# First norm of a fused decoder layer: token tile 0 normalised on VectorE, its first transposes between late output products, and the first FFN block's gate and up products by chunk

## The chip, the core and the metric

The kernel runs on one core of a Trainium2 chip. The core has five engines that work at the same time, each through its own list of instructions in order, and that wait for each other by semaphores: TensorE (PE in the rows) does the matrix products and transposes into PSUM banks, VectorE (DVE) and ScalarE (ACT) do elementwise work, GpSimd (POOL) does some more of it, and SyncE (SP) issues most DMAs. The metric is the device time of one execution in microseconds (us); lower is better. Times in rows are us from the start of the span.

## The reference, cut to what matters

One decoder layer for 256 tokens of width 1024, all in float32: a combined input projection, two groups of attention heads (latent attention and block-sparse attention), an output projection, a first layer norm, a gated FFN with a causal convolution over tokens, and a second layer norm.

```python
mix = jnp.concatenate([a_out, b_out], axis=-1) @ w_o[l]
x = layer_norm(alpha * x + mix, ln1_g[l], ln1_b[l])
x = layer_norm(alpha * x + conv_gated_ffn(x, w_up[l], conv_w[l], conv_b[l], w_down[l]), ln2_g[l], ln2_b[l])

def layer_norm(x, g, b):
    mu = jnp.mean(xf, -1, keepdims=True)
    var = jnp.mean(jnp.square(xf - mu), -1, keepdims=True)
    return (xf - mu) * lax.rsqrt(var + EPS) * g + b

def conv_gated_ffn(x, w_up, conv_w, conv_b, w_down):
    h = x @ w_up                      # 1024 -> 2 * 2816
    h = conv3_causal(h) + conv_b      # each channel over 3 tokens
    gate, up = jnp.split(h, 2, axis=-1)
    return (jax.nn.silu(gate) * up) @ w_down
```

## The kernel before, in words

The 256 tokens are two tiles of 128 (tile 0 and tile 1), the width is eight chunks of 128 columns (`k` from 0 to 7). Each float32 operand of a product is split into a high part (rounded to the fast format float32r) and a low part (what is left), and a product is the sum of three: high by high, low by high, high by low. For weights, `split` (lines 81 to 89) casts the high part on ScalarE and subtracts it on VectorE.

The stage that the change touches lies between the attention and the FFN. Its parts:

- **Output projection** (`gen_wo`, line 414; issued from line 484). The sums `pm` stand in four banks: tile 0 in two halves of 512 columns (`pm00`, `pm0512`), tile 1 likewise (`pm10`, `pm1512`). What is left at the end of attention are the "late" products: line 484 lists those of tile 1, first half of columns for `k` 4 to 7, then second half, and line 485 puts the last chunk of tile 0 (`k` 7, both halves in turn, six products) behind the first two of them.
- **First norm** (lines 495 to 536). For each tile and half, `ln_add` forms `alpha * x + pm` in `r` on VectorE and `ln_part` takes statistics of it; `ln_root` combines them (BN_AGGR on VectorE) and takes a square root on ScalarE; `ln_scale` inverts it on VectorE. Tile 0 is then normalised on ScalarE (lines 530 to 532), tile 1 on VectorE (lines 575 to 577). All of these are pinned: each engine runs them in the order in which they are written (`pin`).
- **Turning the tokens** (class `Turned`, line 538). TensorE transposes chunks of `r` into a bank `x1t`, four chunks to a bank for tile 0 (`a0` for chunks 0 to 3, `a4` for 4 to 7) and two for tile 1 (`tiles[0]` to `tiles[3]`, banks `x1t10`, `x1t12`, `x1t14`, `x1t16`). `affine` multiplies by the norm's gain and adds its bias, from the bank into `x1T` in SBUF, on ScalarE or VectorE; `high` casts `x1T` into the high part `x1hi` on ScalarE; `low` subtracts it into the low part `x1lo`, on GpSimd for tile 0 and on VectorE for tile 1. `keep_warm` puts five products of zeros in front of the transposes of tile 1.
- **FFN** (from line 608). Block `f` of 22 has a gate (`w` 0) and an up part (`w` 1), each with its bank `ph`. In the first block (`f` 0) the products are narrow: 256 columns of `x1hi` for each chunk, then those of `x1lo` (lines 613 to 619). From block 1 on, one product of 512 columns takes `x1hi` and `x1lo` of a chunk together (line 625). `down` (line 669) adds the block's share of the down projection into `pd`, two blocks later.

Except where pinned, a scheduler sets each engine's order in advance; for the first FFN blocks it mixes `ph00`, `ph01` and `ph10` by chunk as their inputs are due. TensorE takes its instructions in that order, so one that waits holds up all behind it.

## Time and profile before

| | |
|---|---|
| time, median of 3 runs | 308.75 us (308.45 to 310.67) |
| profiled execution | 309.6 us, its span 307.8 us |
| TensorE (PE) busy | 296.9 us, 96% of the span |
| VectorE (DVE) busy | 241.9 us, 79% |
| ScalarE (ACT) busy | 196.6 us, 64% |
| GpSimd (POOL) busy | 29.4 us, 10% |

The busy share is an average over stages. The page also slices the span in 40; TensorE shows nine tenths or more in every slice but the first and the last. So the stage in question, some 15 us around 110 us, is to be read from the list of instructions in order of time, engine by engine. In such a row the first number is the start, the second the time from the start of the first to the end of the last instruction of the row, then engine, line of the kernel, operation, what it writes and reads (tile names without their numbers), shape, and count; in brackets, if the engine stood idle before it, how long and for whom it waited. Neighbouring instructions overlap a little: the engine takes the next before the last one's result has landed.

### The profile page before, as it was taken

How to read it: one execution, taken by the hardware profiler on the slowest of the kernel's cores; microseconds unless marked ns; L12 is line 12 of the kernel's file. 1: busy time of each engine (PE TensorE's matmuls, PEld its weight loads, DVE VectorE, ACT ScalarE, POOL GpSimd, SP SyncE). 2: the span in 40 equal slices, each digit the busy share in tenths (PEclk: the TensorE clock that was granted, in tenths of full speed). 3: DMA queues.
4: the chain of work that ended last, by engine and by line, in shares of the span. 5: the costliest groups of instructions: out<-in, count | busy, mean ns of one | idle time of the engine just before them, and what ended most of it. 6: DMA issues, size and time to landing. Idle time of an engine off the chain costs nothing.

```text
span 307.8 us, 4769 instructions
## 1 busy us (share of the span) xinstructions
PE 296.9 (96%) x1672; PEld 258.9 (84%) x1672; DVE 241.9 (79%) x487; ACT 196.6 (64%) x386; POOL 29.4 (10%) x43
## 2 busy tenths in 40 slices
PE   8999999999999989999999999999999999999990
PEld 7987999889887869888888888888888888888890
DVE  2968888866755387999999888888886978975585
ACT  4789797575654287986666657666676768734420
POOL 8330300032320011000000000000000000000021
PEclk9999999999999999999999999999999999999997
DMA  6998866274242103988866566555556776000003
GB/s 205 402 402 276 282 211 204 68 261 148 73 136 75 62 2 106 399 284 252 289 215 185 196 195 197 176 187 178 191 173 201 231 249 204 2 0 0 3 1 137
DMA packets 16217, 54.32 MB, mean 176 GB/s; under 512 B 1824, under 2 KB 2736, under 8 KB 16192
## 3 DMA queue, kind: packets, MB, share of 16 engines
q1 hardware_dynamic: 15840, 52.92, 51.3%
q0 software_dynamic: 352, 1.09, 1.1%
q8 instruction: 13, 0.21, 0.3%
q14 instruction: 12, 0.10, 0.1%
HBM read 52.95 MB, written 1.05 MB: 175 GB/s over the span
## 4 chain that ended last, share of the span: by engine, by line
PE 72%; DVE 14%; DMA 5%; ACT 5%; issue 2%; DVEq 0%; SPq 0%; ACTq 0%
PE ph L625 16%; PE pd L662 12%; PE ph L628 8%; PE pqk L279 7%; PE pm L279 7%; DMA r_wd<-in_w_down 4%; DVE hc L637 4%; PE po L279 4%; PE pv L247 4%; DVE l_wu L88 2%; PE pq L279 2%; PE sca L279 2%; PE scb L279 2%; DVE ld L88 2%; PE pc L181 1%
## 5 line engine op out<-in xcount | busy, mean ns | idle before, releaser
L625 PE MATMUL ph<-x,h_wu 128*128 128x512 f32 x328 | 82.8, 393 | 0.0
L625 PEld LDWEIGHTS ph<-x,h_wu 128*128 128x128 f32 x328 | 59.1, 188 | 10.9
L88 DVE TENSOR_TENSOR l_wu<-r_wu,h_wu 128x1024 fp32r<-128x1024 f32 x44 | 53.6, 1219 | 6.0 <-ACT h_wu L87 5.6
L637 DVE SCALAR_TENSOR_TENSOR hc<-h,cw,hc 128x255 f32<-128x255 f32 x82 | 39.3, 480 | 12.6 <-ACT hc L635 11.7
L87 ACT CAST h_wu<-r_wu 128x1024 fp32r<-128x1024 f32 x44 | 45.8, 1049 | 5.1 <-PE ph L625 3.3
L628 PEld LDWEIGHTS ph<-x,l_wu 128*128 128x128 f32 x328 | 44.7, 190 | 3.4
L628 PE MATMUL ph<-x,l_wu 128*128 128x256 f32 x328 | 45.7, 282 | 0.0
L635 ACT ACTIVATE hc<-h,cw 128x256 f32<-128x256 f32 x41 | 24.6, 601 | 24.1 <-DVE h L632 24.1
L279 PE MATMUL pqk<-x,h_wqk 128*128 128x512 f32 x64 | 20.3, 423 | 0.0
L88 DVE TENSOR_TENSOR l_wd<-r_wd,h_wd 128x1024 fp32r<-128x1024 f32 x16 | 19.5, 1221 | 0.9 <-ACT h_wd L87 0.9
L662 PE MATMUL pd<-l_wd,ghi 128*128 128x512 f32 (+1 forms) x80 | 20.1, 349 | 0.0
L662 PE MATMUL pd<-h_wd,glo 128*128 128x512 f32 (+1 forms) x80 | 20.1, 349 | 0.0
L662 PE MATMUL pd<-h_wd,ghi 128*128 128x512 f32 (+1 forms) x80 | 20.0, 348 | 0.0
L632 DVE TENSOR_TENSOR h<-ph,hb 128x256 f32<-128x256 f32 x41 | 17.1, 417 | 1.9 <-ACT hb L630 1.9
L726 POOL TENSOR_TENSOR r<-r,lnv 128x512 f32<-128x512 f32 x1 | 1.3, 1295 | 181.2 <-ACT r L725 181.2
L87 ACT CAST h_wd<-r_wd 128x1024 fp32r<-128x1024 f32 x16 | 16.7, 1045 | 2.8 <-PE ph L625 2.6
L649 ACT CAST ghi<-gt 128x256 fp32r<-128x256 f32 x22 | 8.9, 404 | 11.7 <-DVE gt L646 11.7
L662 PEld LDWEIGHTS pd<-h_wd,glo 128*128 128x128 f32 x80 | 14.0, 189 | 2.1
L662 PEld LDWEIGHTS pd<-l_wd,ghi 128*128 128x128 f32 x80 | 14.0, 189 | 2.1
L662 PEld LDWEIGHTS pd<-h_wd,ghi 128*128 128x128 f32 x80 | 14.0, 189 | 1.9
L644 ACT ACTIVATE hc<-hc 128x256 f32<-128x256 f32 x22 | 9.1, 414 | 9.8 <-DVE hc L637 9.8
L630 ACT COPY hb<-ph 128x256 f32<-128x256 f32 x41 | 14.9, 363 | 0.0
(167 smaller groups left out, 582.4 us busy)
## 6 DMA issues: line engine op xcount, KB each, us to landing
r_wu<-in_w_up SPq DMA_DIRECT2D x44, 512.0 KB, 3.9
r_wd<-in_w_down SPq DMA_DIRECT2D x22, 512.0 KB, 4.3
r_wqk<-in_w_qk SPq DMA_DIRECT2D x8, 512.0 KB, 4.5
r_wo<-in_w_o SPq DMA_DIRECT2D x8, 512.0 KB, 4.3
r_wv<-in_w_v SPq DMA_DIRECT2D x4, 512.0 KB, 7.6
lnv<-in_ln SPq DMA_DIRECT2D x4, 512.0 KB, 5.4
r_wc<-in_w_c SPq DMA_DIRECT2D x3, 416.0 KB, 6.1
r_wuq<-in_w_uq SPq DMA_DIRECT2D x2, 512.0 KB, 7.8
```

The source lines that it names most:

```text
L87: nc.scalar.copy(hi[:, c], raw[:, c])
L88: nc.vector.tensor_sub(lo[:, c], raw[:, c], hi[:, c].bitcast(F32))
L247: tc.keep_in_program_order(nc.tensor.matmul(pv[t], st[:, k, tk], mv[:, o:o + HALF], start=(k == 0 and i == 0), stop=(k == KT - 1 and i == 2)))
L279: ins = nc.tensor.matmul(*args, **kw)
L625: nc.tensor.matmul(ph, hi[:, ks], x1[:, k].rearrange("p i t -> p (i t)"), start=(k == 0), stop=False)
L628: nc.tensor.matmul(ph[:, :S], lo[:, ks], x1hi[:, k, :], start=False, stop=(k == KT - 1))
L630: nc.scalar.copy(hb, ph[:, S:])
L632: nc.vector.tensor_tensor(h, ph[:, :S], hb, op=ALU.add)
L635: nc.scalar.activation(hc, h, AF.Identity, bias=c[:, 3:4], scale=c[:, 2:3])
L637: nc.vector.scalar_tensor_tensor(hc[:, j:S], h[:, 0:S - j], c[:, 2 - j:3 - j], hc[:, j:S], op0=ALU.mult, op1=ALU.add)
L644: nc.scalar.activation(hg, hg, AF.Silu)
L662: ins = nc.tensor.matmul(pd[t, o][:, :n], st[:, tk], mv[:, o:o + n], start=(f == 0 and i == 0), stop=(f == NF - 1 and i == 2))
```

## The change

Five things change, all between 104 and 122 us.

1. The last chunk of tile 0's output products runs half by half (three products of `pm00`, then three of `pm0512`), and VectorE takes add and statistics half by half instead of both adds, then both statistics.
2. Tile 0 is normalised on VectorE (as tile 1) instead of ScalarE; the small instruction that prepared the shift for ScalarE goes.
3. The last late product group (`k` 7 of tile 1, second half; `TURN` is 7) now stands behind the transposes of `a0`, so that `a0`'s four transposes come before it.
4. ScalarE turns all four chunks of `a0` and casts them before the square root of tile 1; `a4`'s chunks are divided: one on VectorE, two on ScalarE, one on VectorE. For `tiles[0]` the high part comes straight from the bank (`affine_high`, ScalarE); VectorE makes `x1T` of the same two chunks afterwards, for the low part.
5. The first FFN block's gate and up products are written as one loop over chunks (`by_chunk`).

```diff
--- before.py
+++ after.py
@@ -34,7 +34,7 @@
 TURN_AFTER = 4
 LAG = 2
 BEFORE = 2
-A0, A4 = 2, 0
+TURN = 7
 WARM = (6, 5)
 WARM_NARROW = 3
 HELD = 6
@@ -43,7 +43,6 @@
 ATTW_BUFS = 2
 FILL = (8000, 1500, 1500, 1700)
 EARLY = 1
-NARROW = 1
 RES = 8
 RAW_BUFS, HI_BUFS, LO_BUFS = 7, 7, 7
 
@@ -482,7 +481,7 @@
     for t in range(NT):
         nc.gpsimd.dma_start(x_sb[:, t, :], a["x"][:, t, :])
     late = [(k, 1, (grp,)) for grp in COLS[0][1] for k in range(NP, KT)]
-    for k, t, cols in late[:2] + [(KT - 1, 0, None)] + late[2:]:
+    for k, t, cols in late[:2] + [(KT - 1, 0, (grp,)) for grp in COLS[0][0]] + late[2:TURN]:
         run(gen_wo(k, t, cols))
 
     r = acts.tile([P, NT, D], F32, tag="r", name="r")
@@ -522,18 +521,13 @@
     halves = [slice(hf * HALF, (hf + 1) * HALF) for hf in range(2)]
     for hf in range(2):
         ln_add(0, 0, hf, r0, x_sb[:, 0, :], pm)
-    for hf in range(2):
         ln_part(0, 0, hf, r0)
     ln_root(0, 0)
     ln_add(0, 1, 0, r1, x_sb[:, 1, :], pm)
     mu, rs, nm = ln_scale(0, 0)
-    ln_shift(mu, rs, nm)
     for sl in halves:
-        pin(nc.scalar.activation(r0[:, sl], r0[:, sl], AF.Identity, bias=nm, scale=rs))
+        pin(nc.vector.tensor_scalar(r0[:, sl], r0[:, sl], mu, rs, op0=ALU.subtract, op1=ALU.mult))
     ln_part(0, 1, 0, r1)
-    for j in range(1, len(COLS[0][1])):
-        ln_add(0, 1, j, r1, x_sb[:, 1, :], pm)
-        ln_part(0, 1, j, r1)
 
     class Turned:
 
@@ -557,6 +551,13 @@
                     pin(nc.vector.tensor_scalar(dst, src, g1T[:, k:k + 1], b1T[:, k:k + 1],
                                                 op0=ALU.mult, op1=ALU.add))
 
+        def affine_high(self):
+
+            for i in range(self.n):
+                k = self.k0 + i
+                pin(nc.scalar.activation(x1hi[:, k, self.tk], self.ps[:, i * P:(i + 1) * P], AF.Identity,
+                                         bias=b1T[:, k:k + 1], scale=g1T[:, k:k + 1]))
+
         def high(self):
             return pin(nc.scalar.copy(x1hi[:, self.ks, self.tk], self.x1T))
 
@@ -564,27 +565,36 @@
             return pin(eng.tensor_tensor(x1lo[:, self.ks, self.tk], self.x1T,
                                          x1hi[:, self.ks, self.tk].bitcast(F32), op=ALU.subtract))
 
-    a0, a4 = Turned(0, 0, 4, wk_tile), Turned(0, 4, 4, wk_tile)
+    a0 = Turned(0, 0, 4, wk_tile)
+    for k, t, cols in late[TURN:]:
+        run(gen_wo(k, t, cols))
+    a4 = Turned(0, 4, 4, wk_tile)
     keep_warm(WARM[1], "warm1")
-    a0.affine(True, 0, A0)
-    ln_root(0, 1)
-    a0.affine(True, A0)
+    for j in range(1, len(COLS[0][1])):
+        ln_add(0, 1, j, r1, x_sb[:, 1, :], pm)
+        ln_part(0, 1, j, r1)
+    a0.affine(True)
     a0.high()
     a0.low(nc.gpsimd)
-    a4.affine(False, 0, A4)
+    ln_root(0, 1)
+    a4.affine(False, 0, 1)
+    a4.affine(True, 1, 3)
     mu, rs, nm = ln_scale(0, 1)
     for sl in halves:
         pin(nc.vector.tensor_scalar(r1[:, sl], r1[:, sl], mu, rs, op0=ALU.subtract, op1=ALU.mult))
     tiles = [Turned(1, k0, 2, wk_tile if k0 < 4 else acc_tile) for k0 in range(0, KT, 2)]
-    a4.affine(False, A4)
-    tiles[0].affine(True)
-    tiles[0].high()
+    tiles[0].affine_high()
+    a4.affine(False, 3)
+    tiles[0].affine(False)
     a4.high()
     a4.low(nc.gpsimd)
-    for i in range(1, 4):
+    tiles[1].affine(False)
+    tiles[1].high()
+    tiles[0].low(nc.vector)
+    for i in range(2, 4):
         tiles[i].affine(False)
+        last_a = tiles[i].high()
         tiles[i - 1].low(nc.vector)
-        last_a = tiles[i].high()
     last_v = tiles[3].low(nc.vector)
 
     sm.__exit__(None, None, None)
@@ -605,18 +615,30 @@
         with tc.issue_after(last_a.ins), tc.issue_after(last_v.ins):
             return split(raw, n, name)
 
-    def up(f, w):
-        raw = load(a["w_up"][f, :, w, :], CH, f"wu{f}{w}")
-        hi, lo = late_split(raw, CH, f"wu{f}{w}", pin=1 <= f <= 2 and (f, w) != (1, 0))
-        ph = wk_tile(f"ph{f}{w}")
-        if f < NARROW or (f, w) == (NF - 1, 1):
-            for k in range(KT):
-                ks = slice(k * P, (k + 1) * P)
+    def by_chunk(blocks):
+
+        for k in range(KT):
+            ks = slice(k * P, (k + 1) * P)
+            for ph, hi, lo in blocks:
                 nc.tensor.matmul(ph[:, :S], hi[:, ks], x1hi[:, k, :], start=(k == 0), stop=False)
                 nc.tensor.matmul(ph[:, :S], lo[:, ks], x1hi[:, k, :], start=False, stop=False)
-            for k in range(KT):
-                ks = slice(k * P, (k + 1) * P)
+        for k in range(KT):
+            ks = slice(k * P, (k + 1) * P)
+            for ph, hi, lo in blocks:
                 nc.tensor.matmul(ph[:, :S], hi[:, ks], x1lo[:, k, :], start=False, stop=(k == KT - 1))
+
+    ph_first = [wk_tile(f"ph0{w}") for w in range(2)]
+    by_chunk([(ph_first[w], *load_split(a["w_up"][0, :, w, :], CH, f"wu0{w}")) for w in range(2)])
+
+    def up(f, w):
+        ph = ph_first[w] if f == 0 else wk_tile(f"ph{f}{w}")
+        if f:
+            raw = load(a["w_up"][f, :, w, :], CH, f"wu{f}{w}")
+            hi, lo = late_split(raw, CH, f"wu{f}{w}", pin=1 <= f <= 2 and (f, w) != (1, 0))
+        narrow = f == 0 or (f, w) == (NF - 1, 1)
+        if narrow:
+            if f:
+                by_chunk([(ph, hi, lo)])
             h = ph[:, :S]
         else:
 
```

Three places in the instruction lists show the moves. TensorE around the last output products (`pm1512` is tile 1's second half, `x1t00` and `x1t04` are the banks of `a0` and `a4`). Before:

```order
L279 MATMUL pm1512_934<-h_wo6_1160,aTlo_397 128x512
L279 MATMUL pm1512_934<-h_wo7_1181,aThi_396 128x512
L279 MATMUL pm1512_934<-l_wo7_1182,aThi_396 128x512
L279 MATMUL pm1512_934<-h_wo7_1181,aTlo_397 128x512
L548 MATMUL x1t00_1226<-ident_176,r_1209 128x128 x4
L548 MATMUL x1t04_1232<-ident_176,r_1209 128x128 x4
L101 MATMUL warm1_1238<-zero_76 128x128 x5
```

With the change:

```order
L278 MATMUL pm1512_934<-h_wo6_1160,aTlo_397 128x512
L542 MATMUL x1t00_1220<-ident_176,r_1206 128x128 x4
L278 MATMUL pm1512_934<-h_wo7_1181,aThi_396 128x512
L278 MATMUL pm1512_934<-l_wo7_1182,aThi_396 128x512
L278 MATMUL pm1512_934<-h_wo7_1181,aTlo_397 128x512
L542 MATMUL x1t04_1229<-ident_176,r_1206 128x128 x4
L100 MATMUL warm1_1235<-zero_76 128x128 x5
```

The four transposes of `a0` moved ahead of three output products, whose sum tile 1's second half needs.

VectorE from tile 1's combined statistics to the first low part (with what each waits for). Before:

```order
L509 BN_AGGR lnst_1211<-lnst_1211 128x2 [waits DVE_49]
L515 RECIPROCAL lnst_1211<-lnst_1211 128x1 [waits Activation_49]
L577 TENSOR_SCALAR r_1209<-r_1209,lnst_1211 128x512 [waits DVE_49]
L577 TENSOR_SCALAR r_1209<-r_1209,lnst_1211 128x512
L557 TENSOR_SCALAR x1T04_1233<-x1t04_1232,vecs_181 128x128 [waits PE_49]
L557 TENSOR_SCALAR x1T04_1233<-x1t04_1232,vecs_181 128x128 x3
L557 TENSOR_SCALAR x1T12_1260<-x1t12_1259,vecs_181 128x128 [waits PE_49]
L557 TENSOR_SCALAR x1T12_1260<-x1t12_1259,vecs_181 128x128
L564 TENSOR_TENSOR x1_1210<-x1T10_1256,x1_1210 128x2x128 [waits Activation_49]
```

With the change:

```order
L508 BN_AGGR lnst_1208<-lnst_1208 128x2 [waits DVE_49]
L551 TENSOR_SCALAR x1T04_1230<-x1t04_1229,vecs_181 128x128 [waits PE_49]
L514 RECIPROCAL lnst_1208<-lnst_1208 128x1 [waits Activation_49]
L584 TENSOR_SCALAR r_1206<-r_1206,lnst_1208 128x512 [waits DVE_49]
L584 TENSOR_SCALAR r_1206<-r_1206,lnst_1208 128x512
L551 TENSOR_SCALAR x1T04_1230<-x1t04_1229,vecs_181 128x128 [waits Activation_49]
L551 TENSOR_SCALAR x1T10_1258<-x1t10_1257,vecs_181 128x128 [waits Activation_49]
L551 TENSOR_SCALAR x1T10_1258<-x1t10_1257,vecs_181 128x128
L551 TENSOR_SCALAR x1T12_1262<-x1t12_1261,vecs_181 128x128 [waits PE_49]
L551 TENSOR_SCALAR x1T12_1262<-x1t12_1261,vecs_181 128x128
L565 TENSOR_TENSOR x1_1207<-x1T10_1258,x1_1207 128x2x128 [waits DVE_49]
```

The low part of `tiles[0]` (the TENSOR_TENSOR) still follows the chunks of `tiles[1]`, and now also two chunks of `x1T10`, which wait for ScalarE: in the built program that wait stands for the second of ScalarE's two reads of the bank `x1t10`.

TensorE at the first FFN products. Before, then with the change:

```order
L615 MATMUL ph00_1315<-x1_1210,h_wu00_1311 128x256 [waits PE_49,Activation_49]
L616 MATMUL ph00_1315<-x1_1210,l_wu00_1312 128x256
L615 MATMUL ph00_1315<-x1_1210,h_wu00_1311 128x256
L616 MATMUL ph00_1315<-x1_1210,l_wu00_1312 128x256
L615 MATMUL ph01_1350<-x1_1210,h_wu01_1346 128x256
L616 MATMUL ph01_1350<-x1_1210,l_wu01_1347 128x256
L615 MATMUL ph01_1350<-x1_1210,h_wu01_1346 128x256
L616 MATMUL ph01_1350<-x1_1210,l_wu01_1347 128x256
L625 MATMUL ph10_1392<-x1_1210,h_wu10_1388 128x512 [waits DVE_49,Pool_49]
```

```order
L623 MATMUL ph00_1309<-x1_1207,h_wu00_1313 128x256 [waits Activation_49]
L624 MATMUL ph00_1309<-x1_1207,l_wu00_1314 128x256
L623 MATMUL ph01_1310<-x1_1207,h_wu01_1319 128x256 [waits DVE_49]
L624 MATMUL ph01_1310<-x1_1207,l_wu01_1320 128x256
L623 MATMUL ph00_1309<-x1_1207,h_wu00_1313 128x256 [waits Activation_49]
L624 MATMUL ph00_1309<-x1_1207,l_wu00_1314 128x256
L623 MATMUL ph01_1310<-x1_1207,h_wu01_1319 128x256
L624 MATMUL ph01_1310<-x1_1207,l_wu01_1320 128x256
L647 MATMUL ph10_1386<-x1_1207,h_wu10_1389 128x512 [waits DVE_49,Pool_49]
```

The eight narrow products of chunks 0 and 1 now go chunk by chunk, each chunk with its own wait for ScalarE; behind them, in the same place as before, stands the first wide product of block 1 (`ph10`), which reads both parts of chunk 0 and so waits for VectorE's low part of `tiles[0]`.

## Rows read from the trace of the kernel before

**Rows 1.** Busy time by stretch: window, length, engines' busy us, granted clock, DMA.
```profile
115.81:290.00 174.19, 174.19 (x993) 152.58 (x992) 147.16 (x244) 115.50 (x195) 0.90 (x1) 1.00 0.56 182
300.40:303.80 3.40, 0.00 (x0) 0.00 (x0) 3.26 (x8) 0.29 (x1) 0.53 (x1) 1.00 0.42 154
```

**Rows 2.** TensorE in order of time, last output products to first FFN products.
```profile
105.22 0.63 PE L279 MATMUL pm<-h_wo,aTlo 128*128 128x512 f32 x2
...
109.65 0.40 PE L279 MATMUL pm<-h_wo,aTlo 128*128 128x512 f32 x1
110.11 1.36 PE L548 MATMUL x1t<-ident,r 128*128 128x128 f32 x8
111.30 1.28 PE L101 MATMUL warm<-zero 128*128 128x128 f32 x10
113.00 1.07 PE L548 MATMUL x1t<-ident,r 128*128 128x128 f32 x8 [0.42 <-DVE r L577]
114.75 0.39 PE L615 MATMUL ph<-x,h_wu 128*128 128x256 f32 x1 [0.68 <-ACT x L561]
...
115.81 0.40 PE L625 MATMUL ph<-x,h_wu 128*128 128x512 f32 x1
...
121.10 1.55 PE L625 MATMUL ph<-x,h_wu 128*128 128x512 f32 x6
```

**Rows 3.** VectorE in order of time, first norm to low parts.
```profile
105.65 1.28 DVE L498 SCALAR_TENSOR_TENSOR r<-x_sb,pm 128x512 f32<-128x512 f32 x2 [3.37 <-PE pm L279]
...
108.17 0.21 DVE L509 BATCH_NORM_AGGREGATE lnst<-lnst 128x2 f32<-128x12 f32 x1
...
108.85 0.15 DVE L515 RECIPROCAL lnst<-lnst 128x1 f32<-128x1 f32 x1
...
110.09 0.69 DVE L498 SCALAR_TENSOR_TENSOR r<-x_sb,pm 128x512 f32<-128x512 f32 x1 [0.28 <-PE pm L279]
110.81 0.69 DVE L504 BATCH_NORM_STATS2 lnst<-r 128x6 f32<-128x512 f32 x1
111.54 0.21 DVE L509 BATCH_NORM_AGGREGATE lnst<-lnst 128x2 f32<-128x12 f32 x1
112.11 0.17 DVE L515 RECIPROCAL lnst<-lnst 128x1 f32<-128x1 f32 x1 [0.36 <-ACT lnst L510]
112.31 1.00 DVE L577 TENSOR_SCALAR r<-r,lnst 128x512 f32<-128x512 f32 x2
113.23 2.00 DVE L557 TENSOR_SCALAR x1T<-x1t,vecs 128x128 f32<-128x128 f32 x6
115.15 0.41 DVE L564 TENSOR_TENSOR x<-x1T,x 128x256 fp32r<-128x256 f32 x1
...
116.12 0.87 DVE L564 TENSOR_TENSOR x<-x1T,x 128x256 fp32r<-128x256 f32 x1
```

**Rows 4.** ScalarE in order of time, tile 0's norm to high parts.
```profile
109.24 1.52 ACT L532 ACTIVATE r<-r,lnst 128x512 f32<-128x512 f32 x2 [0.53 <-DVE lnst L519]
...
112.81 0.62 ACT L561 CAST x<-x1T 128x512 fp32r<-128x512 f32 x1
113.45 0.81 ACT L555 ACTIVATE x1T<-x1t,vecs 128x128 f32<-128x128 f32 x2
114.29 1.37 ACT L561 CAST x<-x1T 128x256 fp32r<-128x256 f32 x3
```

**Rows 5.** GpSimd in order of time: its two low parts.
```profile
113.51 1.27 POOL L564 TENSOR_TENSOR x<-x1T,x 128x512 fp32r<-128x512 f32 x1 [25.00 <-ACT x L561]
115.32 1.39 POOL L564 TENSOR_TENSOR x<-x1T,x 128x512 fp32r<-128x512 f32 x1 [0.54 <-ACT x L561]
```

**Rows 6.** GpSimd and VectorE in order of time, during attention, around 84 us.
```profile
83.13 1.22 DVE L88 TENSOR_TENSOR l_wo<-r_wo,h_wo 128x1024 fp32r<-128x1024 f32 x1
...
83.37 2.04 POOL L172 TENSOR_SCALAR tab<-dist 128x384 f32<-128x384 f32 x1 [1.97 <-DVE stb L333]
...
84.46 0.60 DVE L341 TENSOR_SCALAR pb<-sb,stb 128x128 f32<-128x128 f32 x2
```

## The prediction, made before the changed kernel was run

> **What bounds the kernel now.** First the busy time by stretch: from 115.81 us, where the first wide FFN product starts, to 290 us TensorE is busy for 174.19 of 174.19 us [rows 1]. So once the FFN runs, nothing off TensorE costs time, and nothing can give time back either: whatever moves the start of that dense stretch moves the end by as much. Then TensorE's list before that point, where its waits stand in brackets or between rows [rows 2]: the last output product starts at 109.65, at its pitch of 0.23 (two in 0.63, one in 0.40) the next would start at 109.89, but the transposes of tile 0 start at 110.11; tile 1's wait 0.42 us for its norm, and the first FFN product 0.68 us for the cast of its first high part. These gaps are all that the change can win: 0.22 + 0.42 + 0.68, and about 0.15 between tile 0's transposes (eight take 1.07 where nothing stops them, 1.36 here), 1.5 us in all, half a per cent. Last the lists of VectorE, ScalarE and GpSimd in the same stretch [rows 3 to 5], since they feed the transposes, the high parts and the low parts.
>
> **The change, part by part.** All clock times are those of the profiled execution; the changed kernel's are worked out on the same axis up to 102 us, where nothing differs.
>
> *Tile 0's norm.* `pm00` gets its last product now at 105.22, the first of that row's two, and the add starts at 105.65, 0.43 later [rows 2, 3]. With the halves one after the other it is the third product of six, not the fifth: 0.47 earlier, so the add starts at 105.18. Add, statistics, add, statistics are then a chain: an add's result is there for its statistics after 0.72 (110.09 to 110.81), statistics for the combination after 0.73 (110.81 to 111.54), and VectorE takes the second add 0.61 after the first statistics start (half of the 1.28 for two, less the overlap) [rows 3]. The combination starts at 105.18 + 0.72 + 0.61 + 0.72 + 0.73 = 107.96, where it is 108.17 now. From there to tile 0's transposes I take what tile 1 needs now for the same steps on VectorE: 111.54 to 113.00, 1.46 [rows 2, 3]. An add of tile 1 stands between combination and inverse (108.17 to 108.85, against 111.54 to 112.11 without it), 0.11 more. So `a0`'s transposes start at 107.96 + 1.46 + 0.11 = 109.53, 0.58 earlier than now. ScalarE loses the two normalising instructions of 1.52 us [rows 4], and they were on the path.
>
> *Late products as filler.* They fill less than meant. The three products that moved behind `a0` started at 109.19 (109.65 less two pitches); now TensorE arrives there, finds `a0`'s input not ready, and waits 109.53 - 109.19 = 0.34. Four transposes take about 0.5 (eight in 1.07, of which 0.27 is the last one's own end). Only then come the three products, so `pm1512` is complete 0.34 + 0.5 = 0.84 later. Tile 1's chain hangs on that sum: add, statistics, combination, root, inverse, norm, 110.09 to 113.00 now [rows 2, 3]. Its transposes start at 113.0 + 0.8 = 113.8. The VectorE instruction put between combination and inverse (0.4) is covered by the root on ScalarE, for which VectorE waits anyway (idle 0.36 there). ScalarE's cast of `a0` ends well before that root is due, at about 112.3.
>
> *First high part from the bank.* Now: transposes 113.00, affine at 113.45, two of them in 0.81, cast of 0.41 at 114.29, product at 114.75 [rows 2, 4]. With the change: transposes 113.8, first affine 114.25 to 114.70, second to 115.06 (pitch 0.36), and the first products need chunk 0 alone. They start at about 114.75, as now; the four of chunk 1 follow at 115.1 (four in 0.48). Dropping the cast (0.41) and waiting for one chunk (0.36) pays just for the 0.8 lost. So far the sum is zero, and the eight narrow products end about when they do now.
>
> *First low part.* This decides. `ph10` stands next and needs `tiles[0]`'s low part. Now that subtraction starts at 115.15, VectorE having had six affines at a pitch of 0.32 (2.00 for six) behind the norm [rows 3]. With the change VectorE must first make `x1T10`, which waits for ScalarE's second read of that bank, until 115.08; then two chunks of it and two of `tiles[1]`, 4 x 0.32, so the subtraction is issued at 116.36. Alone it takes 0.41. But GpSimd will then be in its own subtraction for `a4`: the cast of `a4` follows ScalarE's two affines, 114.97 to 115.59 at 0.62, and GpSimd starts 0.08 behind a cast (112.81 + 0.62 to 113.51) and takes 1.27, until 116.93 [rows 4, 5]. Now the same collision shows at 116.12: a VectorE subtraction issued inside GpSimd's (115.32 to 116.71) took 0.87 instead of 0.41 and ended 0.28 after it [rows 3, 5]. So the low part ends at 116.93 + 0.28 = 117.21 and `ph10` starts at about 117.25, where it starts at 115.81: 1.44 us later. Without the collision it is 116.36 + 0.41 + 0.03 = 116.80, a loss of 1.0. I take 1.44, since the order (GpSimd first) holds by 0.7 us, and keep 1.0 as the lower bound.
>
> *The rest.* Behind `ph10` the later high and low parts come on VectorE and ScalarE at about 1 us per pair of chunks, and TensorE takes about 1 us for each pair, so I see no further stall; I add 0.2 as an upper bound for one. The gate and up products by chunk are the same number and size; the loop costs nothing while TensorE waits for nothing else. The convolution of both parts of block 0 starts together and half a microsecond to a microsecond later than the gate's alone did; its result is used two blocks on (`LAG`), which covers it. SyncE's list has one load of `w_down` moved behind one of the norm's vectors; TensorE's dense stretch begins with loads issued long before.
>
> **The sum.** +0.0 to the first product, +1.44 to the dense stretch, nothing given back. The profiled execution stood at 309.6 us with a span of 307.8; it becomes 311.0. It was 0.85 above the median of the runs, which is what will be compared: 308.75 + 1.44 = 310.2 us, 0.5% slower. One measurement can tell about 1% from no change, so this will hardly be told apart. The range of this case alone: from the bound without collision, less 0.2 for the reading of pitches, to 1.44 + 0.2 and 0.4 of spread between medians: 309.5 to 310.8.
>
> **A rule against a row.** On the path stands also VectorE's norm of tile 1 (two TENSOR_SCALAR from SBUF to SBUF), at about 113.1, while GpSimd is in its subtraction for `a0` (112.4 to 113.7, since the cast of `a0` ends earlier than now). The nearest row is of attention: two TENSOR_SCALAR issued at 84.46, inside GpSimd's 83.37 to 85.41, took 0.60 for both, unhindered, while GpSimd's own instruction was the long one (2.04), after a two-operand subtraction of VectorE that ran to 84.35 [rows 6]. So I charge nothing. The Trainium skill (SBUF — State Buffer, section Who interferes with whom) says that a `tensor_scalar` of VectorE can take both ports, and then whichever of VectorE and GpSimd starts second stands still until the other ends. By that rule the first half of the norm would end at 113.7 + 0.27 instead of 113.65, 0.3 later, and the sum would be 310.5; the row at 84.46 speaks against it here.
>
> **The rivals.**
>
> *Faster: the low part is in time.* If `a0`'s input is ready when TensorE arrives, tile 1 loses 0.5 instead of 0.8, and if `tiles[0]`'s low part ends before TensorE has done the eight narrow products, the gap of 0.68 us before the first product [rows 2] is the prize: 308.75 - 0.68 = 308.1. The turning point is whether the low part ends before about 115.7. Against it: the wait for ScalarE's second read at about 115.06, four affines and a subtraction are 1.7 us of work behind it. Chance 0.13.
>
> *No difference.* The two effects are each half as large as I make them (affines from the bank faster, VectorE waiting less): within 0.4 of 308.75. Chance 0.13.
>
> *The port rule holds.* VectorE's norm is held up by GpSimd as above: 310.5. For it, the norm moves into GpSimd's stretch, where it did not lie before; against it, the row at 84.46. Chance 0.1.
>
> *The clock falls.* TensorE would stand idle twice, 1.3 us before tile 1's transposes (warm products end at about 112.5) and 1.5 us before `ph10`, within 5 us. If the granted clock went from 2.4 to 1.2 GHz there, the mostly narrow products that now take 5.3 us (115.81 to 121.10) [rows 2] would take twice that: 308.75 + 1.44 + 5.3 = 315.5. Against it: after its last product TensorE does nothing from 300.40 to 303.80 and the granted clock is still 1.00 [rows 1]. Chance 0.03.
>
> **Numbers.** Forecast 0.61, port rule 0.1, no difference 0.13, faster 0.13, clock 0.03. Predicted 310.2. The range goes from 308.4 (the likeliest case, the port rule, most of no difference; it leaves out the faster case) to 311.2 (port rule and spread on top). Faster by over 1% would need 305.7, twice what all the gaps hold: 0.01. Slower by over 1% is 311.8: the clock, and a stall that I have not seen: 0.06. Within 1%: 0.93.
>
> **What would show it.** In the changed profile: `a0`'s transposes at about 109.5, and an idle stretch of 0.3 before them; tile 1's transposes near 113.8 with a longer wait for VectorE than 0.42; the first FFN product near 114.75 with a wait for ScalarE of at most 0.2; then a new wait of TensorE before the first wide product, 1.0 to 1.5 us, ended by VectorE's subtraction, and that subtraction lasting about 0.85 with GpSimd's around it. If that wait is missing, the forecast is wrong; if tile 1's transposes come at 113.0 or earlier, the charge for the late products is.

## The result, and the profile after

The changed kernel takes 311.25 us (median of 20 executions, 310.37 to 312.42), the kernel before in 20 executions of its own 309.41 us (308.19 to 310.80). The ratio is 1.0059 with a 95% interval from 1.0044 to 1.0074: 1.83 us slower (1.4 to 2.3), where 1.44 was forecast, 310.2 us in all. Of the 1.05 us between the forecast time and the measured one, 0.66 us is the starting value (the median of the three executions known when the prediction was made, 308.75, lay low against that of the twenty) and 0.39 the change itself.

The time of one execution also holds what happens in its first 20 us, so the traces are compared by **the stretch**: from the first of the last 24 output products of tile 0 and tile 1 (in the kernel before they start within 5.36 us of each other) to the first down product `pd`. In the kernel before its two ends are these rows of TensorE in order of time, 27.53 us apart:

```profile
104.29 0.63 PE L279 MATMUL pm<-h_wo,aThi 128*128 128x512 f32 x2
...
131.82 0.63 PE L662 MATMUL pd<-h_wd,ghi 128*128 128x512 f32 x2
```

The page of the changed kernel begins with busy time and share of the span (308.7 us, in an execution of 310.45). The two rows below it are TensorE's busy share in the 40 slices of the span, first of the kernel before, then of the changed one:

```profile
PE 294.1 (95%) x1672; PEld 257.1 (83%) x1672; DVE 243.0 (79%) x488; ACT 195.8 (63%) x385; POOL 29.5 (10%) x43
...
PE   8999999999999989999999999999999999999990
...
PE   6999999999999978999999999999999999999990
```

So in the kernel before not every slice but the first and the last has nine tenths: the 15th, from 107.7 to 115.4 us, has eight, and it is the one in which the change works. In the changed kernel that slice has seven and the next eight.

TensorE of the changed kernel in order of time, against [rows 2]:

```profile
103.72 0.40 PE L278 MATMUL pm<-h_wo,aThi 128*128 128x512 f32 x1
...
108.95 0.63 PE L542 MATMUL x1t<-ident,r 128*128 128x128 f32 x4 [0.17 <-DVE r L529]
...
110.56 1.28 PE L100 MATMUL warm<-zero 128*128 128x128 f32 x10
113.55 1.06 PE L542 MATMUL x1t<-ident,r 128*128 128x128 f32 x8 [1.71 <-DVE r L584]
114.50 0.39 PE L623 MATMUL ph<-x,h_wu 128*128 128x256 f32 x1
...
117.08 0.48 PE L647 MATMUL ph<-x,h_wu 128*128 128x512 f32 x1 [1.37 <-DVE x L565]
...
133.14 0.63 PE L684 MATMUL pd<-h_wd,ghi 128*128 128x512 f32 x2
```

The stretch is 133.14 - 103.72 = 29.42 us, 1.89 longer. Counted from its start: tile 1's transposes 9.83 (before 8.71), first FFN product 10.78 (10.46), first wide product 13.36 (11.52), `pd` 29.42 (27.53). So 1.84 of the 1.89 us are there when the wide product starts, behind a new wait of 1.37 us for VectorE. Behind it TensorE is busy without a break, as in [rows 1]; the second row below is the time after its last product:

```profile
117.08:290.00 172.92, 172.92 (x985) 151.66 (x986) 146.69 (x244) 116.05 (x195) 0.00 (x0) 1.00 0.55 183
301.20:304.60 3.40, 0.00 (x0) 0.00 (x0) 3.26 (x8) 0.30 (x1) 0.57 (x1) 0.98 0.42 154
```

VectorE of the changed kernel, against [rows 3]: the norm of tile 1, an affine of `a4`, the two affines of `x1T10` and two of `tiles[1]` behind a wait for ScalarE's read of the bank, and `tiles[0]`'s low part:

```profile
112.54 1.31 DVE L584 TENSOR_SCALAR r<-r,lnst 128x512 f32<-128x512 f32 x2
113.78 0.40 DVE L551 TENSOR_SCALAR x1T<-x1t,vecs 128x128 f32<-128x128 f32 x1
114.83 1.37 DVE L551 TENSOR_SCALAR x1T<-x1t,vecs 128x128 f32<-128x128 f32 x4 [0.66 <-ACT x L558]
116.12 0.82 DVE L565 TENSOR_TENSOR x<-x1T,x 128x256 fp32r<-128x256 f32 x1
```

GpSimd of the changed kernel, against [rows 5], its low parts of `a0` and `a4`:

```profile
111.86 1.26 POOL L565 TENSOR_TENSOR x<-x1T,x 128x512 fp32r<-128x512 f32 x1 [23.91 <-ACT x L562]
115.39 1.27 POOL L565 TENSOR_TENSOR x<-x1T,x 128x512 fp32r<-128x512 f32 x1 [2.27 <-ACT x L562]
```

Two instructions of VectorE start inside GpSimd's and are long for it. The two halves of the norm take 1.31 us instead of 1.00 [rows 3]; the subtraction at 116.12 takes 0.82 instead of 0.41 and ends at 116.94, 0.28 after GpSimd's (115.39 + 1.27). In the norm it is the first half that is long, 0.86 us instead of 0.55; it ends at 113.40, and GpSimd's subtraction at 113.12.

### The profile page after: what moved, and what is told of

Read it like the earlier page. It is cut to its first block, busy times and chain, and to the rows that moved or that the text cites. A ratio compares the mean times of both kernels' runs of the same rounds, so it can differ in the third digit from the quotient of the medians.

```text
span 308.7 us, 4767 instructions
## 1 busy us (share of the span) xinstructions
PE 294.1 (95%) x1672; PEld 257.1 (83%) x1672; DVE 243.0 (79%) x488; ACT 195.8 (63%) x385; POOL 29.5 (10%) x43
## 3 DMA queue, kind: packets, MB, share of 16 engines
HBM read 52.95 MB, written 1.05 MB: 175 GB/s over the span
## 4 chain that ended last, share of the span: by engine, by line
PE 89%; DVE 6%; DMA 2%; ACT 1%; issue 1%; SPq 0%; DVEq 0%
PE ph L647 25%; PE pd L684 18%; PE ph L650 13%; PE pqk L278 7%; PE pm L278 6%; PE pv L246 4%; PE po L278 4%; PE pq L278 2%; DMA r_wc<-in_w_c 2%; PE sca L278 2%; PE scb L278 2%; DVE r L497 1%; DVE lnst L503 1%; PE pc L181 1%; PE ph L628 1%; DVE r L733 1%
```

## The experiments

In all of them the stretch is measured in the profiled execution, from rows of TensorE like those above. Each mark is from one profiled execution; how far the stretch repeats is seen where an edit turned out to cost nothing: 27.54 beside 27.53 (e10_before_byc), 29.42 beside 29.42 (e13_warm). The table gives its marks, in us from its start; the sections below have the kernels' names in their headings.

| kernel | tile 1's transposes | first FFN product | first wide product | `pd` |
|---|---|---|---|---|
| before | 8.71 | 10.46 | 11.52 | 27.53 |
| changed | 9.83 | 10.78 | 13.36 | 29.42 |
| e1_pool_held | 9.50 | 10.46 | 13.04 | 29.08 |
| e2_both_held | 9.52 | 10.48 | 12.65 | 29.11 |
| e4_no_filler | 10.17 | 11.48 | 13.72 | 29.86 |
| e10_before_byc | 8.72 | 10.46 | 11.52 | 27.54 |
| e3_no_bank | 9.82 | 11.57 | 18.70 | 29.88 |
| e3w_warm | 9.83 | 11.58 | 17.82 | 28.99 |
| e8_before_filler | 10.12 | 11.86 | 13.62 | 30.39 |
| e8w_warm | 10.13 | 11.88 | 12.94 | 28.94 |
| e16_no_filler_root | 8.96 | 10.49 | 13.08 | 31.22 |
| e16w_warm | 8.96 | 10.49 | 13.07 | 29.12 |
| e12_wide_behind | 9.83 | 10.79 | 18.30 | 29.47 |
| e13_warm | 9.84 | 10.80 | 13.38 | 29.42 |
| b4_high_first | 8.71 | 9.67 | 15.73 | 26.90 |
| e19w_high_first | 9.84 | 10.80 | 16.77 | 27.94 |

### GpSimd held once (e1_pool_held)

```diff
     a0.high()
-    a0.low(nc.gpsimd)
...
         pin(nc.vector.tensor_scalar(r1[:, sl], r1[:, sl], mu, rs, op0=ALU.subtract, op1=ALU.mult))
+    pin(nc.gpsimd.tensor_copy(held_t[:, 0:1], r1[:, D - 1:D]))
+    a0.low(nc.gpsimd)
```

> The changed kernel with one thing added: GpSimd's low part of tile 0's first half waits until VectorE has normalised tile 1. Measured is the stretch from the first product of tile 0's last chunk to the first product of pd (before: 104.29 to 131.82, 27.53 us; changed: 103.72 to 133.14, 29.42 us). Theory (port hold): the first half of the norm of tile 1 takes 0.55 us instead of 0.86, tile 1's transposes come at 9.52 instead of 9.83 us of the stretch, and all behind them moves by as much: first wide product at 13.05 instead of 13.36, stretch 29.1 us. Rival (the norm's length is off the path, something else ends last at the wide product): the norm takes 0.55 but the stretch stays at 29.4. Rival (the hold is not GpSimd's doing): the norm still takes 0.86 us.

Measured: 29.08 us, the wide product at 13.04. The norm on VectorE of this kernel:

```profile
112.63 1.01 DVE L584 TENSOR_SCALAR r<-r,lnst 128x512 f32<-128x512 f32 x2
```

It takes what it took in the kernel before (1.00 us), tile 1's transposes come 0.33 us earlier, and 0.34 us reach the end. The hold is GpSimd's doing and lies on the path.

### GpSimd held twice (e2_both_held)

```diff
+    pin(nc.gpsimd.tensor_copy(held_t[:, 0:1], r1[:, D - 1:D]))
+    a0.low(nc.gpsimd)
...
     tiles[0].low(nc.vector)
+    pin(nc.gpsimd.tensor_copy(held_t[:, 1:2], x1lo[:, 0, 2 * P - 1:2 * P].bitcast(F32)))
+    a4.low(nc.gpsimd)
```

> The changed kernel with both of GpSimd's low parts held: the first until VectorE has normalised tile 1, the second until VectorE has made tiles[0]'s low part. Theory (two collisions, both on the path to the first wide product): the norm loses 0.31 us and the subtraction that ends at the wide product takes 0.41 instead of 0.82 us, so the first wide product starts at 13.36 - 0.31 - 0.41 = 12.64 us of the stretch and pd's first product at 29.42 - 0.72 = 28.7 us; the remaining 1.2 us over the 27.53 of the kernel before belong to VectorE's work ahead of that subtraction and to the late start of tile 1. Rival (the wait only moves to the next chunk's high part): the first wide product comes at 12.6 but the stretch stays above 29.0. Rival (GpSimd is the whole cause): 27.5 to 27.9 us.

Measured: the wide product at 12.65, as the theory said, but the end at 29.11, no earlier than with one hold: the first rival. VectorE of this kernel shows where it went:

```profile
115.66 0.41 DVE L566 TENSOR_TENSOR x<-x1T,x 128x256 fp32r<-128x256 f32 x1
115.99 0.72 DVE L552 TENSOR_SCALAR x1T<-x1t,vecs 128x128 f32<-128x128 f32 x2
116.63 1.22 DVE L566 TENSOR_TENSOR x<-x1T,x 128x256 fp32r<-128x256 f32 x1
```

GpSimd and TensorE, which has a wait that was not there:

```profile
116.28 1.30 POOL L566 TENSOR_TENSOR x<-x1T,x 128x512 fp32r<-128x512 f32 x1
...
118.99 0.38 PE L626 MATMUL ph<-x,h_wu 128*128 128x256 f32 x1 [0.16 <-ACT x L563]
```

GpSimd's subtraction now runs from 116.28 to 117.58 and holds the next subtraction of VectorE, 1.22 us instead of 0.41, and through it the high part of the last two chunks, for which TensorE waits. The collision was moved and not removed. With this my theory that the subtraction's 0.41 us are part of the end fell: TensorE meets the late conversions at the wide product or a little later, with the same sum.

### Late products ahead of the transposes again (e4_no_filler)

```diff
-TURN = 7
+TURN = 8
```

> The changed kernel with no late product behind tile 0's transposes: the last three stand ahead of them again, as in the kernel before. Theory (tile 0's transposes fall late by the three products, 0.7 us, and ScalarE's affines and cast of tile 0, which took until 111.78 of the changed run, then run into the root of tile 1 that VectorE wants at 111.3): tile 1's add comes some 0.7 us earlier, its root waits for the cast until about 112.5, and nothing is won: stretch 29.4 to 29.9 us against 29.42. Rival (the late products behind the transposes are the cause, since pm1512 is complete 0.84 us later for them): 29.42 - 0.84 = 28.6 us.

Measured: 29.86 us. The granted clock was 0.78 from 112 to 116 us and 0.80 from 116 to 120, so the end is not a clean number; what rules the rival out is the start of tile 1's transposes, at 10.17 us and not earlier than the changed kernel's 9.83, behind a wait for VectorE. Tile 1's combination comes early and its root waits for ScalarE's cast of `a0`; the norm then starts inside GpSimd's subtraction (112.22 to 113.48) 0.9 us before that ends, and takes 1.65 us:

```profile
112.22 1.26 POOL L565 TENSOR_TENSOR x<-x1T,x 128x512 fp32r<-128x512 f32 x1 [24.26 <-ACT x L562]
...
112.37 0.16 DVE L514 RECIPROCAL lnst<-lnst 128x1 f32<-128x1 f32 x1 [0.65 <-ACT lnst L509]
112.57 1.65 DVE L584 TENSOR_SCALAR r<-r,lnst 128x512 f32<-128x512 f32 x2
```

The root is ready at the same 8.60 us of the stretch as in the changed kernel: one delay hides the other.

### Gate and up by chunk, alone (e10_before_byc)

```diff
...
+    ph_first = [wk_tile(f"ph0{w}") for w in range(2)]
+    by_chunk([(ph_first[w], *load_split(a["w_up"][0, :, w, :], CH, f"wu0{w}")) for w in range(2)])
...
```

> The kernel before with one part of the change: gate and up of the first FFN block together, chunk by chunk. Theory (the loop costs and wins nothing by itself, since TensorE issues the same products in the same stretch, and the first high part still comes from the cast): first wide product at 11.5 us of the stretch, first product of pd at 27.5 us, as in the kernel before. Rival (the order by chunk costs the time, because the up half's products come late for the convolution or the wide product stands behind more work): 28.0 to 29.4 us.

Measured: 27.54 us, first wide product 11.52. In the kernel before this part is free.

### The first high part as before (e3_no_bank, e3w_warm)

```diff
-    tiles[0].affine_high()
+    tiles[0].affine(True)
+    tiles[0].high()
     a4.affine(False, 3)
-    tiles[0].affine(False)
```

> The changed kernel with the high part of tiles[0] made as in the kernel before: ScalarE's affine into x1T and a cast, no second read of that bank by VectorE. Same stretch as in the earlier runs (changed kernel 29.42 us to pd's first product, before 27.53). Theory (the second reading of the bank sits on VectorE, whose list is what TensorE waits for): the first FFN product comes 0.8 us later (1.75 us behind tile 1's first transpose, as in the kernel before, so at 9.83 + 1.75 = 11.6 us instead of 10.78), yet VectorE is rid of the wait of 0.66 us and of two affines of 0.32, and the end comes 0.3 to 0.7 us earlier: 28.7 to 29.1 us. Rival (the first product sets the end): 29.42 + 0.8 = 30.2 us. Rival (the bank is the whole loss): 27.5 to 27.8.

Measured: first FFN product 11.57 as expected, but 29.88 us; the granted clock between 112 and 120 us was 0.75 and 0.82, so this run did not decide. It was repeated with TensorE kept busy ahead of tile 1's transposes (`WARM = (6, 10)`):

> The changed kernel with the high part of tiles[0] made as in the kernel before, as in the earlier run of that, and ten instead of five products on zeros before tile 1's transposes. The earlier run had the first FFN product at 11.57 us of the stretch and a granted clock of 0.75 and 0.82 from 112 to 120 us, and took 29.88 us. Theory (the high part from the bank costs more on VectorE than it saves; the clock took the rest of the earlier run): at a full clock 28.9 to 29.1 us, 0.3 to 0.5 less than the changed kernel, though the first FFN product is 0.8 us later. Rival (the high part from the bank is worth its 0.8 us): 29.8 us or more at a full clock.

Measured: 28.99 us at a granted clock of 1.00. The first FFN product comes 0.8 us later and the end 0.43 earlier: in this order the new high part costs more on VectorE than it saves on ScalarE. Two other things differ in these two runs: the scheduler put the first wide product behind the products by chunk (18.70 and 17.82 in the table), and the second run has more products on zeros. In the changed kernel itself neither moves the end (29.47 in e12_wide_behind, 29.42 in e13_warm).

### Late products behind the transposes, alone (e8_before_filler, e8w_warm)

```diff
-    for k, t, cols in late[:2] + [(KT - 1, 0, None)] + late[2:]:
+    for k, t, cols in late[:2] + [(KT - 1, 0, None)] + late[2:7]:
...
-    a0, a4 = Turned(0, 0, 4, wk_tile), Turned(0, 4, 4, wk_tile)
+    a0 = Turned(0, 0, 4, wk_tile)
+    for k, t, cols in late[7:]:
+        run(gen_wo(k, t, cols))
+    a4 = Turned(0, 4, 4, wk_tile)
...
```

> The kernel before with one part of the change: the last three late products stand behind a0's transposes. Theory (late products behind a wait delay pm1512 and with it tile 1's whole chain): a0's transposes cannot start before 110.11 in the trace of before, whatever stands ahead; four of them take 0.5 us and the three products 0.7, so pm1512 is complete at about 111.4 instead of 110.05, tile 1's transposes come 1.2 to 1.5 us later, nothing behind them catches up, and the stretch is 28.7 to 29.0 us instead of 27.53. Rival (what costs time in the changed kernel is only the wait before the wide product; late products are filler and cost nothing): 27.5 to 27.8 us.

Measured: tile 1's transposes at 10.12, as expected, but 30.39 us. Its busy times by stretch have the granted clock third from the end:

```profile
112.00:116.00 4.00, 2.16 (x18) 1.76 (x17) 3.54 (x11) 2.64 (x7) 1.01 (x1) 1.00 0.02 4
116.00:120.00 4.00, 3.77 (x18) 3.67 (x19) 3.86 (x11) 2.39 (x6) 1.62 (x2) 0.57 0.00 0
```

Between 116 and 120 us that is close to the lower of the two levels (1.2 of 2.4 GHz). TensorE had stood idle for 0.75, 1.40 and 0.68 us between 109.4 and 116.23. The run was repeated with four more products on zeros:

> The kernel before with the last three late products behind a0's transposes, as in the earlier run of that, and nine instead of five products on zeros before tile 1's transposes. The earlier run came out at 30.39 us of the stretch instead of 28.7 to 29.0, with tile 1's transposes at 10.12 (as expected, 1.40 later than in the kernel before) and a granted clock of 0.57 between 116 and 120 us. Theory (1.4 us are the late transposes, the rest is the clock): with a granted clock of 1.00 the stretch is 28.8 to 29.1 us. Rival (the rest is another wait): 30.2 to 30.4 at a full clock. If the clock falls all the same, the run tells nothing about this.

```profile
112.00:116.00 4.00, 2.81 (x24) 2.42 (x23) 3.57 (x11) 3.27 (x8) 1.27 (x1) 1.00 0.02 4
116.00:120.00 4.00, 4.00 (x33) 3.87 (x33) 3.25 (x9) 2.38 (x5) 1.39 (x1) 1.00 0.00 0
```

Measured: 28.94 us, all of it at full clock. Late products cost 1.40 us by themselves in the kernel before, and the clock had taken another 1.45.

### Tile 1 early in the changed kernel (e16_no_filler_root, e16w_warm)

```diff
-TURN = 7
+TURN = 8
...
-    a0.affine(True)
+    a0.affine(True, 0, 2)
+    ln_root(0, 1)
+    a0.affine(True, 2)
     a0.high()
     a0.low(nc.gpsimd)
-    ln_root(0, 1)
```

> The changed kernel without late products behind a0's transposes and with tile 1's root on ScalarE ahead of a0's last two affines and cast, as in the kernel before. Tile 1's transposes then come at about 9.0 us of the stretch instead of 9.83 (pm1512 complete 0.84 earlier, the root not kept waiting). Theory (ScalarE's and VectorE's conversions set the end, not TensorE's transposes; what ScalarE no longer does before the root it does after it): the end moves by less than half of that, to 28.9 to 29.2 us. Rival (the late start of tile 1 carries through to the end): 29.42 - 0.84 = 28.5 us or less.

Measured: 31.22 us, with tile 1's transposes at 8.96 and a granted clock of 0.81, 0.50 and 0.84 in the three stretches of 4 us from 112 to 124. It was repeated with three more products on zeros:

> The changed kernel without late products behind a0's transposes and with tile 1's root early, as in the earlier run of that, and eight instead of five products on zeros before tile 1's transposes. The earlier run had tile 1's transposes at 8.96 us of the stretch and the first wide product at 13.08, but a granted clock of 0.81, 0.50 and 0.84 in the three stretches of 4 us from 112 to 124, and the stretch took 31.22 us. Theory (conversions set the end; the clock took the rest): at a full clock the first wide product stays at 13.0 to 13.1 and the stretch is 28.9 to 29.2 us. Rival (the late start of tile 1 carries through to the end): 28.5 us or less at a full clock. If the clock falls all the same (there is a second idle time of 0.86 us before the wide product), the stretch stays above 30.

Measured at a granted clock of 1.00: wide product 13.07, end 29.12. Tile 1 is 0.87 us earlier than in the changed kernel and the end only 0.30: what ScalarE and VectorE have to convert sets it. The first FFN product waits for ScalarE there (0.47 us), whose instructions follow each other with hardly a break from 111.30 to 114.86 us, since the affines and the cast that no longer stand ahead of the root now stand behind it.

### The wide product behind the products by chunk (e12_wide_behind)

```diff
...
-            for k in range(KT):
-                ks = slice(k * P, (k + 1) * P)
-                nc.tensor.matmul(ph, hi[:, ks], x1[:, k].rearrange("p i t -> p (i t)"), start=(k == 0), stop=False)
+            with tc.issue_after(by_chunk.last.ins) if (f, w) == (1, 0) else nullcontext():
+                for k in range(KT):
+                    ks = slice(k * P, (k + 1) * P)
+                    nc.tensor.matmul(ph, hi[:, ks], x1[:, k].rearrange("p i t -> p (i t)"), start=(k == 0), stop=False)
```

> The changed kernel with the products of the wide block ph10 kept behind all products by chunk of the first block, so that TensorE does not stand at tiles[0]'s low part. Theory (VectorE's and ScalarE's conversions set the end; the wait before the wide product is only where TensorE meets them): TensorE waits for the casts of tiles[1] and tiles[2] instead; in the changed run these end at 12.92 and 14.30 us of the stretch, the products of the chunks before them at 11.95 and about 13.9, so 0.97 + 0.4 = 1.4 us of waits come in place of the 1.37, and the stretch stays at 29.3 to 29.6 us. Rival (the place of the wide product is the fault, the order of TensorE's work): 29.42 - 1.4 = 28.0 us.

Measured: 29.47 us, the wide product at 18.30. TensorE of this kernel waits for two casts instead:

```profile
117.75 0.39 PE L623 MATMUL ph<-x,h_wu 128*128 128x256 f32 x1 [0.97 <-ACT x L562]
...
119.13 0.39 PE L623 MATMUL ph<-x,h_wu 128*128 128x256 f32 x1 [0.16 <-ACT x L562]
```

So the place of the wide product is not the fault.

### The clock in the changed kernel (e13_warm)

```diff
-WARM = (6, 5)
+WARM = (6, 10)
```

> The changed kernel with ten instead of five products on zeros between tile 0's and tile 1's transposes (20 matrix passes instead of 10, 2.5 us instead of 1.28), so that TensorE is busy until shortly before tile 1's transposes at 113.55; all other work is the same. Of the 20 executions of the changed kernel 11 had a mean granted clock of 0.991 to 0.996 (median 310.83 us) and 9 one of 0.986 or 0.987 (median 311.58 us). Theory (in part of the executions the clock falls behind the idle 1.71 us): the lower group of clocks disappears, the median comes to about 310.8 us, 1.4 us above the kernel before, and in the trace the stretch stays at 29.4 us with a granted clock of 1.00 from 108 to 124 us. Rival (the two groups have nothing to do with this place, and the whole 1.84 us is the wait for the conversions): median 311.2 to 311.4 and the group at 0.987 is still there.

Measured: 311.33 us (6 executions against 17 of the kernel before at 308.57; ratio 1.0077, 1.0057 to 1.0097), the stretch 29.42, and a mean clock of 0.987 is still there in two of the six: the theory fell. In the trace of this kernel, itself one of 0.987, the clock is lower in the first 20 us and full in the stretch:

```profile
0.00:20.00 20.00, 17.62 (x77) 15.99 (x78) 10.56 (x23) 12.10 (x31) 11.51 (x27) 0.91 0.90 321
108.00:124.00 16.00, 13.86 (x100) 12.40 (x99) 12.45 (x29) 9.83 (x20) 2.54 (x2) 1.00 0.13 29
```

That lies 80 us ahead of the first instruction that the change moves.

### High parts first (b4_high_first, e19w_high_first)

The kernel before with gate and up by chunk, `affine_high`, one affine of `a4` between combination and inverse, the wide block behind the products by chunk, and this order of conversions:

```diff
...
-    a4.affine(False, A4)
-    tiles[0].affine(True)
-    tiles[0].high()
+    tiles[0].affine_high()
+    a4.affine(False, 1, 3)
+    tiles[1].affine(False)
+    tiles[1].high()
+    a4.affine(False, 3)
     a4.high()
+    tiles[2].affine(False)
+    tiles[2].high()
     a4.low(nc.gpsimd)
-    for i in range(1, 4):
-        tiles[i].affine(False)
-        tiles[i - 1].low(nc.vector)
-        last_a = tiles[i].high()
-    last_v = tiles[3].low(nc.vector)
+    tiles[3].affine(False)
+    last_a = tiles[3].high()
+    tiles[0].affine(False)
+    for i in range(4):
+        last_v = tiles[i].low(nc.vector)
...
```

> A version meant to be faster than both kernels: the first norm and the late products as in the kernel before; gate and up of the first block together by chunk; the first high part straight from the bank on ScalarE; VectorE makes the affines of all high parts first and the low parts after them, and the products of the wide block stand behind those by chunk, so that no low part is needed early. Theory (what counts is when the conversions come on VectorE; in the changed kernel the early low part and x1T10 held them up): tile 1's transposes at 8.7 us of the stretch as in the kernel before, first FFN product 0.95 us behind them as in the changed kernel, at 9.7 instead of 10.46, no wait over 0.2 behind it, pd's first product at 26.8 to 27.0 us against 27.53: 0.5 to 0.7 us faster than the kernel before. Rival (the high parts of the later chunks cannot come any faster, so the gain turns into a wait before the second or third chunk): 27.4 to 27.6, no difference.

Measured: 308.02 us against 308.57 (12 and 17 executions), ratio 0.9982, 95% from 0.9966 to 0.9999, so a gain of 0.2% that only just clears no change; the stretch is 26.90 us, 0.63 less than before. VectorE of this kernel, and GpSimd's second subtraction:

```profile
113.13 1.01 DVE L584 TENSOR_SCALAR r<-r,lnst 128x512 f32<-128x512 f32 x2
114.05 3.59 DVE L557 TENSOR_SCALAR x1T<-x1t,vecs 128x128 f32<-128x128 f32 x11
117.67 1.43 DVE L571 TENSOR_TENSOR x<-x1T,x 128x256 fp32r<-128x256 f32 x4
...
116.46 1.30 POOL L571 TENSOR_TENSOR x<-x1T,x 128x512 fp32r<-128x512 f32 x1 [0.84 <-ACT x L568]
```

Eleven affines and four subtractions run without a break at 0.33 and 0.36 us each, though GpSimd works from 114.33 to 115.61 and from 116.46 to 117.76. The affines, which read a bank, are not held, and the subtractions start 0.09 us before GpSimd is done.

The same order in the changed kernel (with `WARM = (6, 10)`):

```diff
     tiles[0].affine_high()
-    a4.affine(False, 3)
-    tiles[0].affine(False)
-    a4.high()
-    a4.low(nc.gpsimd)
     tiles[1].affine(False)
     tiles[1].high()
-    tiles[0].low(nc.vector)
-    for i in range(2, 4):
-        tiles[i].affine(False)
-        last_a = tiles[i].high()
-        tiles[i - 1].low(nc.vector)
-    last_v = tiles[3].low(nc.vector)
+    a4.affine(False, 3)
+    a4.high()
+    tiles[2].affine(False)
+    tiles[2].high()
+    a4.low(nc.gpsimd)
+    tiles[3].affine(False)
+    last_a = tiles[3].high()
+    tiles[0].affine(False)
+    for i in range(4):
+        last_v = tiles[i].low(nc.vector)
```

> The changed kernel with the conversions in the order of the faster version (affines of all high parts first on VectorE, x1T10 and the low parts behind them) and ten instead of five products on zeros, so that the clock stays out of it; late products, first norm and first high part as in the changed kernel. Theory (the loss is made of two things that add: tile 1 starts 1.12 us late, and the conversions' order): from tile 1's first transpose to pd's first product the faster version needs 26.90 - 8.71 = 18.19 us; tile 1's transposes stay at 9.83, so pd comes at 28.0 us of the stretch instead of 29.42, and 1.4 us of the changed kernel's loss are the order, 1.1 the late start (the new first high part gives back 0.6). Rival (the order only helps where tile 1 starts early; here ScalarE's casts or GpSimd's collisions set the end): 28.6 us or more.

Measured: 27.94 us, the wide product at 16.77. So the order of the conversions alone is worth 29.42 - 27.94 = 1.48 us of the changed kernel's loss. The remaining 27.94 - 26.90 = 1.04 to the version above goes with the later start of tile 1 (9.84 instead of 8.71, the hold of the norm included), but these two kernels also differ in tile 0's norm and in how `a4` is divided, and no run takes these apart. The version above is in its turn 0.63 ahead of the kernel before. That 1.48 + 1.04 - 0.63 gives 1.89 is bookkeeping between four runs and no further proof, and it holds for this order of steps: in the changed kernel's own order of conversions a start of tile 1 that was 0.87 us earlier was worth 0.30 at the end (e16w_warm).

## Why the prediction was right and wrong

- **Tile 0's norm** was right: `a0`'s transposes start 5.23 us into the stretch, 0.59 earlier than before (5.82), where 0.58 was said.
- **Late products as filler** was right in kind: 0.8 us were charged to tile 1's start, and with the hold of the norm taken out it is 0.79 (9.50 less 8.71). The run of this part alone shows it as a cost of 1.40 us in the kernel before, where `a0` is ready later. What the prediction did not say is that ScalarE's cast of `a0` stood ready to take its place (e4_no_filler).
- **"So I charge nothing"** is the step that failed. The norm of tile 1 and GpSimd's subtraction were put in the same place and the hold was priced at zero, by a row of attention [rows 6]. It measured 0.31 us at the norm and 0.34 at the end (e1_pool_held). Its own rival, the port rule with a chance of 0.1, had 0.3 for it and is what happened: 1.44 + 0.3 = 1.74 us, where 1.83 were measured. The Trainium skill (SBUF — State Buffer, section Who interferes with whom) has VectorE and GpSimd shut each other out when VectorE's `tensor_scalar` takes both ports. For this pair the traces agree: the first half of the norm ends 0.28 us after GpSimd in the changed kernel (113.40 and 113.12) and as long after it in the run without late products (e4_no_filler). That a port is the reason no run here shows. The row that was set against it was also read too smoothly. The two instructions of [rows 6] (128x128 and 128x256) took 0.60 us, but 0.54 at 89.93 us with GpSimd idle; and GpSimd's instruction, long there with 2.04 us, took 1.17 in five other places and had started inside VectorE's subtraction, so that it seems to have waited itself. Why the two were not held to GpSimd's end at 85.41 is open: they are shorter than the norm's halves and GpSimd's was another operation; it was not tried.
- **First high part from the bank**: the first FFN product was reckoned at 0 and came 0.32 later, which is the hold again: with the hold out of the way it comes at 10.46, as in the kernel before (e1_pool_held).
- **First low part**: mechanism, place and both causes were right (the wait for the second read of the bank, four affines, GpSimd's collision at 0.82 us, where the row had 0.87). The wide product came 1.84 us later where 1.44 was said: 0.31 from the hold, and 0.1 between the subtraction's end at 116.94 and the product at 117.08, where 0.04 was allowed. But the bound without collision, 1.0, was no bound of the end: without it (e2_both_held against e1_pool_held) the wide product came 0.39 earlier and the end did not.
- **Dense behind it** was right for the changed kernel: TensorE busy 172.92 of 172.92 us. That whatever moves the start of the dense stretch moves the end by as much was not: in e12_wide_behind the wide product starts 4.94 us later than in the changed kernel and the end comes 0.05 later.
- **The clock** was given 0.03 for a reason that does not carry: [rows 1] show a clock of 1.00 in idle time at the end, and the row that answers to it now shows 0.98. In the changed kernel's trace the clock stayed at 1.00 over waits of 1.71 and 1.37 us. In four traces of its neighbours it fell in this place (e3, e4, e8 and e16), and in three of them a repeat with more products on zeros took 0.89, 1.45 and 2.10 us less. How many of the 20 timed executions of the changed kernel had it is not known.
- **The starting value**: the kernel before had a median of 308.75 in three executions, 309.41 in twenty and 308.57 in another seventeen. The largest of these differences, 0.84, is more than twice the failed term, and the allowance for spread between medians was 0.4. With 309.41 to start from, the same sum would have said 310.85.

## What to carry to other kernels

In this stage a wait was where TensorE met the late work, and not the cause: taking away the collision at the wide product, or the wide product itself, moved the wait and left the end. What paid lay ahead of it on VectorE: 0.34 us for the norm without its hold, and 1.48 for another order of VectorE's list (everything that TensorE needs first, all low parts last). When a step is moved to VectorE, look at what GpSimd does at that moment, and price the overlap by a row with the same pair of operations and sizes. Work put behind a wait as filler comes later by that wait and by what stands in front of it, and so does whoever needs its result: 0.8 us here, 1.40 in the kernel before.

## What the runs showed that was not expected

- A TENSOR_SCALAR of VectorE from SBUF to SBUF (128x512) that starts while GpSimd is in a TENSOR_TENSOR ends 0.28 us after GpSimd does: first halves of the norm of 0.86 and 1.19 us instead of 0.55, with GpSimd done 0.58 and 0.91 after VectorE's start (changed kernel and e4_no_filler). TENSOR_SCALARs that read a bank kept their 0.33 us inside GpSimd's stretches (b4_high_first).
- The sum of idle time does not tell when the clock falls: waits of 1.71 and 1.37 us passed at a granted clock of 1.00 in the changed kernel, waits of 0.75, 1.40 and 0.68 us ended at 0.57 in another (e8_before_filler).
- The high part made straight from the bank cost 0.43 us in one order of the conversions (e3w_warm) and is part of a gain of 0.63 in another (b4_high_first); what it is worth by itself there no run shows.
